# The recurrence inputs of a decoder step, made a second time by shifted columns of the stationary operand

## The chip, the cores and the metric

The kernel runs on one core of a Trainium2 chip. The metric is the device time of one execution in microseconds; the number given for a kernel is the median of its runs. All times below are microseconds (us) unless they are marked ns.

## What is computed

One layer of a hybrid decoder trunk, for a prompt of 1024 tokens and a decode batch of 8 sequences with 8 tokens each. A combined input projection feeds a dilated sliding-window attention and an S5 state-space group; their outputs are normalised, joined, projected, and a SwiGLU feed-forward part follows. The change is in the state-space part, which has 32 groups of 64 complex states and 16 channels each:

```python
def _cmul_combine(e1, e2):
    a1r, a1i, b1r, b1i = e1
    a2r, a2i, b2r, b2i = e2
    ...
    br = a2r * b1r - a2i * b1i + b2r
    bi = a2r * b1i + a2i * b1r + b2i
    return ar, ai, br, bi

def _s5(u, h0_re, h0_im, ...):
    ...
    bu_re = jnp.einsum('btgc,gnc->btgn', uf, bb_re)
    bu_im = jnp.einsum('btgc,gnc->btgn', uf, bb_im)
    ...
    _, _, h_re, h_im = lax.associative_scan(_cmul_combine, (a_r, a_i, bu_re, bu_im), axis=1)
    y = (jnp.einsum('btgn,gcn->btgc', h_re, c_re) - jnp.einsum('btgn,gcn->btgc', h_im, c_im) + d_skip * uf)
```

## The kernel before

The program has three phases. Phase A normalises the tokens, makes the input projection, and builds the tables of the state-space part. Phase B runs the prompt attention (`prompt_attn`) beside the recurrence (`ssm_main`), and after it the gate of the state-space output (`ssm_gate`) and the decode attention's values (`sample_values`). Phase E is the output projection and the feed-forward part, and takes more than half of the span.

Generators yield after each small step, and `merge` interleaves them by weights. That gives every instruction a priority; a scheduler then puts the instructions of each engine into a fixed order, engine by engine, with semaphores between engines. Every engine runs its own instructions in that order, and the DMA issues all stand in one queue, that of SyncE.

The recurrence runs over chunks of 8 tokens, 128 chunks of the prompt and 8 of the decode batch, so that an input tile U has 8 + 128 = 136 columns per group. Its 32 groups are 8 units u of 4 groups (one set of loads WI, WO, T, CS each), and each unit has two pairs m of 2 groups: 16 pairs. In SBUF and PSUM the 128 partitions hold the real rows (0 to 63) and the imaginary rows (64 to 127) of the states. A pair goes through five stages, one step apart, in `ssm_main`:

- `s0`: matmuls of the stationary WI (128 columns per group) with U give the chunk inputs in one PSUM bank px (tag `sd`, three banks for all users). The first pair of a unit also prepares HS on GpSimd.
- `s1`: ScalarE copies the 8 decode columns to xs (L928). VectorE multiplies the 128 prompt columns by a cosine table (L929, all 128 partitions), and by a sine table with real and imaginary rows exchanged, in two instructions on 64 partitions each (L930, L931). GpSimd subtracts (L932).
- `s2`: VectorE scans along the chunks (L940); GpSimd rotates back (L941 to L944).
- `s3`: the sum goes to HS (L948), on GpSimd or VectorE.
- `s4`: matmuls with T and WO give the outputs; ScalarE copies them to Y (L963).

All these matmuls have f32 operands, and each is recorded as two rows of weight load and two of matmul. `loads(u)` fetches the tables of a unit; WI has two buffers, so that the load of unit u waits for the last read of unit u - 2. Before the first load, the decode state is loaded in two halves through one buffer `hb`, transposed on PE and kept as h0. The line of every matmul is L75 (`mm1`), that of every transpose L79 (`tr`), of a load L82 and of a split L64 and L65, since helpers issue them.

The functions that the change touches, as the profile numbers their lines:

Of the kernel before, what the change touches and what calls it, by code (L numbers as in the profile page):

```python
# [10 lines left out]
F32 = mybir.dt.float32  # L11
F32R = mybir.dt.float32r
I32 = mybir.dt.int32
AF = mybir.ActivationFunctionType
OP = mybir.AluOpType
# [19 lines left out]
PB, VB, VSB, KKB, PTB, TAB, TCB, HSB, UB, CSB, WSB, HB = 10, 6, 4, 2, 2, 3, 2, 3, 2, 3, 5, 5  # L35
# [11 lines left out]
class K:  # L47
# [837 lines left out]
    def ssm_main(self, sp):  # L885
        nc, I, O = self.nc, self.I, self.O
        V, G = nc.vector, nc.gpsimd
        P8 = self.P8
        xs = sp.tile([128, 8, 32], F32, name="xs")
        hf = sp.tile([128, 32], F32, name="hf")  # L890
        WI, WO, T, CS, U, HS, Y, px, ta, tb, tcc = ({} for _ in range(11))

        def loads(u):
            if u >= 8:
                return
            q = u // 2
            if u % 2 == 0:
                U[q] = sp.tile([128, 8, 136], F32, tag="U", name="U", bufs=UB)
                self.load(U[q], self.dU[128 * q:128 * q + 128].rearrange("(g c) s t -> (c s) g t", c=16))
            WI[u] = sp.tile([128, 4, 128], F32, tag="WI", name="WI", bufs=2)  # L900
            WO[u] = sp.tile([128, 4, 128], F32, tag="WO", name="WO", bufs=3)
            T[u] = sp.tile([128, 4, 128], F32, tag="T", name="T", bufs=3)
            c = CS[u] = sp.tile([128, 2, 4, 128], F32, tag="CS", name="CS", bufs=CSB)
            self.load(WI[u], self.dWI[u])
            for h in range(2):
                self.load(c[64 * h:64 * h + 64].rearrange("p a g t -> p (a g t)"), self.dCS[q][64 * (u % 2):64 * (u % 2) + 64, h])
            self.load(T[u], self.dT[q][:, 4 * (u % 2):4 * (u % 2) + 4])
            self.first = self.load(WO[u], self.dWO[u])

        def s0(m):  # L910
            u, pr = divmod(m, 2)
            if pr == 0:
                HS[u] = sp.tile([128, 4, 138], F32, tag="HS", name="HS", bufs=HSB)
                G.memset(HS[u][:, :, 8:9], 0.0)
                G.tensor_scalar(HS[u][:, :, 0:8], h0[:, 0, :, 4 * u:4 * u + 4].rearrange("p b g -> p g b"), 1.0, 0.0, op0=OP.mult, op1=OP.add)
            px[m] = self.bank("sd")
            for j in range(2):
                g = 2 * pr + j
                self.mm1(px[m][:, 136 * j:136 * j + 136], WI[u][:, g], U[u // 2][:, 4 * (u % 2) + g])

        def s1(m):
            u, pr = divmod(m, 2)
            pxv = px[m][:, 0:272].rearrange("p (g c) -> p g c", g=2)
            co, si = CS[u][:, 0, 2 * pr:2 * pr + 2], CS[u][:, 1, 2 * pr:2 * pr + 2]
            a = ta[m] = sp.tile([128, 2, 128], F32, tag="ta", name="ta", bufs=TAB)
            b = tb[m] = sp.tile([128, 2, 128], F32, tag="tb", name="tb", bufs=TAB)
            g0 = 4 * u + 2 * pr
            nc.scalar.activation(xs[:, :, g0:g0 + 2].rearrange("p b g -> p g b"), pxv[:, :, 0:8], AF.Copy)  # L928
            V.tensor_tensor(a, pxv[:, :, 8:136], co, op=OP.mult)  # L929
            V.tensor_tensor(b[0:64], pxv[64:128, :, 8:136], si[64:128], op=OP.mult)  # L930
            V.tensor_tensor(b[64:128], pxv[0:64, :, 8:136], si[0:64], op=OP.mult)  # L931
            G.tensor_tensor(out=a, in0=a, in1=b, op=OP.subtract)  # L932

        def s2(m):
            u, pr = divmod(m, 2)
# [31 lines left out]

        h0 = sp.tile([128, 2, 8, 32], F32, name="h0")
        for half in range(2):
            hb = sp.tile([128, 3, 64], F32, tag="hb", name="hb", bufs=1)  # L970
            self.load(hb[:, 1], I["state_ssm_re"][0].rearrange("b g n -> (b g) n")[128 * half:128 * half + 128])
            self.load(hb[:, 2], I["state_ssm_im"][0].rearrange("b g n -> (b g) n")[128 * half:128 * half + 128])
            V.tensor_scalar(hb[:, 0], hb[:, 2], -1.0, None, op0=OP.mult)
            pt = self.bank("sd")
            self.tr(pt[:, 0:128], hb[:, 1:3].rearrange("p a n -> p (a n)"))
            self.tr(pt[:, 128:256], hb[:, 0:2].rearrange("p a n -> p (a n)"))
            nc.scalar.activation(h0[:, :, 4 * half:4 * half + 4].rearrange("p a b g -> p a (b g)"), pt[:, 0:256].rearrange("p (a c) -> p a c", a=2), AF.Copy)
        loads(0)
        yield 0
        for m in range(20):  # L980
            for k, f in enumerate((s0, s1, s2, s3, s4)):
                if 0 <= m - k < 16:
                    f(m - k)
            if m % 2 == 1:
                loads(m // 2 + 1)
            yield 3.0
# [1060 lines left out]
```

## Time and profile before

| | |
|---|---|
| median of three runs | 1548.5 us (1545.07 to 1552.62) |
| the profiled execution | 1555.69 us, of which the span is 1553.6 |
| granted TensorE clock, mean of the span | 0.939 of full speed |
| PE busy | 1439.5 us (93%) |
| PE weight loads busy | 1344.9 us (87%) |
| VectorE busy | 1090.4 us (70%) |
| ScalarE, GpSimd busy | 716.1 and 729.1 us (46%, 47%) |

PE is TensorE's matmul side and PEld its weight loads, DVE is VectorE, ACT ScalarE, POOL GpSimd, SP SyncE. A busy share is the time covered by recorded instructions. Matmuls are pipelined, so that a busy PE is not a PE at its peak; the distance between the starts of successive rows tells more. The granted clock is given as a share of 2.4 GHz; 0.50 is the lower level of 1.2 GHz. The recurrence stage discussed here lies between 316 and 446 us of the span.

### The profile page before, as it was taken

The page shows a single profiled execution, that of the slowest core. Times are in us where ns is not written, and L with a number is a line of the kernel's source. Part 1 is how long each engine was busy: PE and PEld are TensorE (multiplying, and loading weights), DVE is VectorE, ACT ScalarE, POOL GpSimd, SP SyncE. Part 2 cuts the span into 40 slices and gives each one's busy share as a digit, 9 for nine tenths or more (in the row PEclk, how much of TensorE's full clock was granted, in tenths as well). Part 3 has the DMA queues.
Part 4 walks back from the last instruction along what each step waited for, and adds up shares of the span by engine and source line. Part 5 has one row for each costly group of instructions (what it writes and reads, how often), then busy time and mean ns, then how long its engine had stood idle before and what let it go on. Part 6 is the DMA issues. An engine that isn't in the chain of part 4 may idle for free.

```text
span 1553.6 us, 28199 instructions
## 1 busy us (share of the span) xinstructions
PE 1439.5 (93%) x10005; PEld 1344.9 (87%) x10005; DVE 1090.4 (70%) x2226; ACT 716.1 (46%) x1815; POOL 729.1 (47%) x719
## 2 busy tenths in 40 slices
PE   5988987978889999999997999999999989999996
PEld 5987977966777677789987999999999989999996
DVE  6896399958867787787989555555555577579564
ACT  6233343435467667575444333333232365466443
POOL 3058445417735454410147678788774421113331
PEclk9998988968789999889998999999999999999998
DMA  8438887799676873444342276566564368689874
GB/s 215 160 120 279 242 241 220 209 214 224 179 189 180 206 182 89 127 146 128 108 131 80 84 214 212 175 205 196 184 197 141 108 248 294 195 297 324 238 234 126
DMA packets 244187, 292.90 MB, mean 189 GB/s; under 512 B 29870, under 2 KB 185358, under 8 KB 244046
## 3 DMA queue, kind: packets, MB, share of 16 engines
q1 hardware_dynamic: 244046, 291.10, 62.7%
q8 instruction: 79, 1.29, 0.4%
q14 instruction: 62, 0.51, 0.1%
HBM read 211.69 MB, written 79.35 MB: 187 GB/s over the span
## 4 chain that ended last, share of the span: by engine, by line
PE 60%; DVE 11%; DMA 7%; issue 4%; ACT 2%; POOL 1%; SPq 1%; POOLq 0%; DVEq 0%; ACTq 0%
PE pmm L72 15%; PE pmm L70 15%; PE pmm L71 15%; PE psd L75 5%; PE pmm L75 3%; PE ptr L79 2%; PE ppo L75 2%; DVE kk L682 1%; SPq L82 1%; DMA kk<-in_cache_attn_k_dram 1%; DVE ws L65 1%; PE ptr L75 1%; DMA hs<-dH 1%; DMA kf<-in_cache_attn_k_dram 1%; DVE hn L65 1%
## 5 line engine op out<-in xcount | busy, mean ns | idle before, releaser
L70 PE MATMUL pmm<-hn,ws 128*128 128x272 f32 x1232 | 359.1, 292 | 9.1 <-DVE u L1775 4.6
L72 PE MATMUL pmm<-hn,ws 128*128 128x272 f32 x1232 | 358.2, 291 | 2.1 <-DVE ws L65 2.1
L71 PE MATMUL pmm<-hn,ws 128*128 128x272 f32 x1232 | 356.9, 290 | 0.8 <-DVE hn L65 0.8
L64 ACT ACTIVATE ws<-wr 128x512 fp32r<-128x512 f32 (+2 forms) x238 | 151.8, 645 | 207.4 <-PE pmm L72 191.0
L70 PEld LDWEIGHTS pmm<-hn,ws 128*128 128x128 f32 x1232 | 234.1, 190 | 10.5 <-DVE u L1775 4.8
L65 DVE TENSOR_TENSOR ws<-wr,ws 128x512 fp32r<-128x512 f32 (+2 forms) x238 | 202.4, 857 | 52.7 <-ACT ws L64 51.3
L72 PEld LDWEIGHTS pmm<-hn,ws 128*128 128x128 f32 x1232 | 233.6, 190 | 2.9 <-DVE ws L65 2.7
L71 PEld LDWEIGHTS pmm<-hn,ws 128*128 128x128 f32 x1232 | 234.1, 190 | 1.3 <-DVE hn L65 1.2
L70 PE MATMUL pmm<-hs,ws 128*128 128x272 f32 x448 | 131.5, 294 | 5.1 <-DVE hid L1772 5.1
L72 PE MATMUL pmm<-hs,ws 128*128 128x272 f32 x448 | 131.2, 295 | 0.5 <-DVE ws L65 0.5
L71 PE MATMUL pmm<-hs,ws 128*128 128x272 f32 x448 | 131.3, 294 | 0.0
L1779 POOL TENSOR_TENSOR hid<-hid,s 128x272 f32<-128x272 f32 x88 | 82.2, 941 | 55.9 <-DVE hid L1772 52.0
L65 DVE TENSOR_TENSOR ws<-st,ws 128x512 fp32r<-128x512 f32 x72 | 60.6, 842 | 59.0 <-ACT ws L64 58.8
L828 POOL TENSOR_TENSOR vs<-vr,vs 128x512 fp32r<-128x512 f32 x40 | 56.0, 1406 | 85.3 <-ACT vs L826 75.1
L681 POOL TENSOR_TENSOR kf<-kf,qb 128x1024 f32<-128x1024 f32 x24 | 59.1, 2471 | 73.0 <-DMA kf<-in_cache_attn_k_dram 37.3
L70 PEld LDWEIGHTS pmm<-hs,ws 128*128 128x128 f32 x448 | 86.1, 192 | 5.3 <-ACT hs L64 5.3
L72 PEld LDWEIGHTS pmm<-hs,ws 128*128 128x128 f32 x448 | 85.5, 192 | 0.9 <-DVE ws L65 0.8
L71 PEld LDWEIGHTS pmm<-hs,ws 128*128 128x128 f32 x448 | 86.0, 192 | 0.0
L64 ACT ACTIVATE ws<-st 128x512 fp32r<-128x512 f32 x72 | 45.3, 629 | 81.0 <-PE pmm L72 69.9
L1125 DVE CUSTOM_DVE_ANT_0 P<-pmm,lnc 128x256 f32<-128x256 f32 (+1 forms) x128 | 47.4, 376 | 41.9 <-PE pmm L75 33.6
L70 PE MATMUL pmm<-mT,ws 128*128 128x272 f32 x256 | 74.5, 298 | 1.4 <-ACT ws L64 1.4
L71 PE MATMUL pmm<-mT,ws 128*128 128x272 f32 x256 | 74.9, 295 | 0.0
(441 smaller groups left out, 4088.3 us busy)
## 6 DMA issues: line engine op xcount, KB each, us to landing
vr<-in_cache_attn_v_dram SPq DMA_DIRECT2D x80, 256.0 KB
wr<-dS SPq DMA_DIRECT2D x32, 512.0 KB
hs<-dH SPq DMA_DIRECT2D x28, 544.0 KB
kf<-in_cache_attn_k_dram SPq DMA_DIRECT2D x48, 256.0 KB
wr<-in_ffn_w_gate_dram SPq DMA_DIRECT2D x24, 512.0 KB
wr<-in_ffn_w_up_dram SPq DMA_DIRECT2D x24, 512.0 KB
wx<-dS SPq DMA_DIRECT2D x24, 512.0 KB
dH<-hid SPq DMA_DIRECT2D x22, 544.0 KB
```

The costliest lines, as they stand in the source:

```text
L64: self.nc.scalar.activation(hi, src, AF.Copy)
L65: (eng or self.nc.vector).tensor_tensor(out=lo, in0=src, in1=raw(hi), op=OP.subtract)
L70: nc.tensor.matmul(out, lhsT=wh, rhs=xh, start=start, stop=False)
L71: nc.tensor.matmul(out, lhsT=wh, rhs=xl, start=False, stop=False)
L72: nc.tensor.matmul(out, lhsT=wl, rhs=xh, start=False, stop=stop)
L75: self.nc.tensor.matmul(out, lhsT=w, rhs=x, start=start, stop=stop)
L79: self.nc.tensor.transpose(out, in_, self.ident[:n, :n])
L82: return self.nc.sync.dma_start(out=out, in_=in_).ins
L681: nc.gpsimd.tensor_tensor(out=kf[i], in0=kf[i], in1=qb[b][:, 0:1].to_broadcast((128, 2, 512)), op=OP.mult)
L828: eng.tensor_tensor(out=s[:, 1], in0=vr[i], in1=raw(s[:, 0]), op=OP.subtract)
L1125: V.tensor_tensor_reduce(out=P[h, g].rearrange("p b k -> p (b k)")[:, o:o + n], in0=s[:, o:o + n], in1=lnc[:, part, 256 - n:256], scale=-1 ...
L1779: self.mark = G.tensor_tensor(out=o, in0=o, in1=sb, op=OP.mult).ins
```

## The change

The input matmuls of a pair are made twice. WI gets 64 more columns per group, a copy of its first 64, made by ScalarE in SBUF once per unit. Columns 0 to 127 are the stationary operand of the first product, as before; columns 64 to 191 are that of the second, whose output has real and imaginary rows exchanged. Both products cover the 128 prompt columns alone and lie side by side in one PSUM bank of 512 columns. VectorE then multiplies each by its table on all 128 partitions, and GpSimd adds where it subtracted. The 8 decode columns get matmuls of their own, four per unit, in a bank of their own, with one ScalarE copy per unit instead of one per pair. The tile `hb` moves into the slots of the tag `ta`, of which there are three, so that the two halves have a slot each.

```diff
-            WI[u] = sp.tile([128, 4, 128], F32, tag="WI", name="WI", bufs=2)
+            WI[u] = sp.tile([128, 4, 192], F32, tag="WI", name="WI", bufs=2)
...
-            self.load(WI[u], self.dWI[u])
+            self.load(WI[u][:, :, 0:128], self.dWI[u])
...
                 G.tensor_scalar(HS[u][:, :, 0:8], h0[:, 0, :, 4 * u:4 * u + 4].rearrange("p b g -> p g b"), 1.0, 0.0, op0=OP.mult, op1=OP.add)
+                nc.scalar.activation(WI[u][:, :, 128:192], WI[u][:, :, 0:64], AF.Copy)
+                p = self.bank("sd")
+                for g in range(4):
+                    self.mm1(p[:, 8 * g:8 * g + 8], WI[u][:, g, 0:128], U[u // 2][:, 4 * (u % 2) + g, 0:8])
+                nc.scalar.activation(xs[:, :, 4 * u:4 * u + 4].rearrange("p b g -> p g b"), p[:, 0:32].rearrange("p (g b) -> p g b", g=4), AF.Copy)
+
             px[m] = self.bank("sd")
-            for j in range(2):
-                g = 2 * pr + j
-                self.mm1(px[m][:, 136 * j:136 * j + 136], WI[u][:, g], U[u // 2][:, 4 * (u % 2) + g])
+            for k in range(2):
+                for j in range(2):
+                    g = 2 * pr + j
+                    self.mm1(px[m][:, 256 * k + 128 * j:256 * k + 128 * j + 128], WI[u][:, g, 64 * k:64 * k + 128], U[u // 2][:, 4 * (u % 2) + g, 8:136])
...
-            pxv = px[m][:, 0:272].rearrange("p (g c) -> p g c", g=2)
+            pxv = px[m].rearrange("p (k g c) -> p k g c", k=2, g=2)
...
-            g0 = 4 * u + 2 * pr
-            nc.scalar.activation(xs[:, :, g0:g0 + 2].rearrange("p b g -> p g b"), pxv[:, :, 0:8], AF.Copy)
-            V.tensor_tensor(a, pxv[:, :, 8:136], co, op=OP.mult)
-            V.tensor_tensor(b[0:64], pxv[64:128, :, 8:136], si[64:128], op=OP.mult)
-            V.tensor_tensor(b[64:128], pxv[0:64, :, 8:136], si[0:64], op=OP.mult)
-            G.tensor_tensor(out=a, in0=a, in1=b, op=OP.subtract)
+            V.tensor_tensor(a, pxv[:, 0], co, op=OP.mult)
+            V.tensor_tensor(b, pxv[:, 1], si, op=OP.mult)
+            G.tensor_tensor(out=a, in0=a, in1=b, op=OP.add)
...
-            hb = sp.tile([128, 3, 64], F32, tag="hb", name="hb", bufs=1)
+            hb = sp.tile([128, 2, 128], F32, tag="ta", name="hb", bufs=TAB).rearrange("p a (b n) -> p (a b) n", n=64)
```

## Rows read from the trace of the kernel before

**Rows 1.** The page: the chain that ended last, share of the span by engine.
```profile
PE 60%; DVE 11%; DMA 7%; issue 4%; ACT 2%; POOL 1%; SPq 1%; POOLq 0%; DVEq 0%; ACTq 0%
```
**Rows 2.** Windows: length; PE, PEld, DVE, ACT, POOL busy (instructions); clock, DMA share, GB/s.
```profile
335.00:355.00 20.00, 15.58 (x66) 12.79 (x65) 13.38 (x35) 6.68 (x23) 8.56 (x14) 0.59 1.07 232
355.00:375.00 20.00, 17.57 (x93) 14.34 (x93) 19.51 (x62) 9.32 (x35) 16.61 (x26) 0.86 0.84 200
375.00:395.00 20.00, 20.00 (x117) 16.64 (x114) 16.01 (x55) 12.26 (x42) 12.22 (x24) 0.91 0.80 221
395.00:415.00 20.00, 16.14 (x84) 13.69 (x84) 18.16 (x52) 6.62 (x24) 16.21 (x27) 0.83 0.87 221
415.00:432.00 17.00, 16.79 (x60) 13.00 (x60) 11.66 (x32) 9.29 (x26) 10.94 (x19) 0.50 0.60 147
```
**Rows 3.** Waits, 335 to 440 us: us in total, times, longest.
```profile
PE psd L75 <- DMA WI<-dWI: 6.1, 1, 6.1
PE psd L75 <- DVE tb L940: 3.3, 1, 3.3
PE pmm L75 <- DVE ST L1125: 0.6, 2, 0.4
```
**Rows 4.** Groups by line, 335 to 432 us: busy, mean ns, idle before and releaser.
```profile
L931 DVE TENSOR_TENSOR tb<-psd,CS 64x256 f32<-64x256 f32 x16 | 6.7, 417 | 0.2
L929 DVE TENSOR_TENSOR ta<-psd,CS 128x256 f32<-128x256 f32 x16 | 6.6, 411 | 1.4 <-ACT xs L928 1.1
L928 ACT ACTIVATE xs<-psd 128x16 f32<-128x16 f32 x16 | 3.1, 193 | 10.3 <-PE psd L75 10.3
```
**Rows 5.** Timeline of VectorE: start, us, instruction.
```profile
347.90 0.42 DVE L1125 CUSTOM_DVE_ANT_0 P<-pmm,lnc 128x256 f32<-128x256 f32 x1
...
348.25 0.42 DVE L1125 CUSTOM_DVE_ANT_0 P<-pmm,lnc 128x256 f32<-128x256 f32 x1
...
389.25 0.42 DVE L930 TENSOR_TENSOR tb<-psd,CS 64x256 f32<-64x256 f32 x1
389.69 0.42 DVE L931 TENSOR_TENSOR tb<-psd,CS 64x256 f32<-64x256 f32 x1
```
**Rows 6.** Timeline of PE's matmuls, with the idle time before in brackets.
```profile
356.68 1.25 PE L75 MATMUL psd<-U,WI 128*128 128x136 f32 x4 [6.10 <-DMA WI<-dWI]
357.72 0.66 PE L75 MATMUL psd<-U,T 128*128 128x136 f32 x2
...
396.31 0.68 PE L75 MATMUL psd<-U,WI 128*128 128x136 f32 x4
396.75 0.98 PE L75 MATMUL ppo<-PT,VS 128*128 128x128 f32 x7
```
**Rows 7.** The tile WI: count, ns minimum/median/maximum, first and last start.
```profile
L75 PE MATMUL psd<-U,WI x64: 277/407/594, 334.1 to 411.5; 128*128 128x136 f32 x64
```
**Rows 8.** Timeline of PE's weight loads for selection matmuls of 16 columns.
```profile
311.11 1.42 PEld L75 LDWEIGHTS psd<-sel,Z 128*128 128x128 f32 x12
...
339.07 1.82 PEld L75 LDWEIGHTS psd<-sel,Z 128*128 128x128 f32 x12
```
**Rows 9.** Timeline of ScalarE.
```profile
329.53 0.50 ACT L1135 ACTIVATE P<-P,ST 128x256 f32<-128x256 f32 x1
```
**Rows 10.** Timeline of SyncE's queue around the loads of hb.
```profile
322.12 1.82 SPq L82 DMA_DIRECT2D CS<-dCS  x2
328.65 0.34 SPq L82 DMA_DIRECT2D hb<-in_state_ssm_re_dram  x1
```
**Rows 11.** Windows of 2 us, with the columns of the second group.
```profile
326.00:328.00 2.00, 2.00 (x5) 1.25 (x5) 1.52 (x6) 1.97 (x3) 0.00 (x0) 0.50 1.11 291
328.00:330.00 2.00, 2.00 (x6) 1.27 (x5) 0.73 (x4) 2.00 (x9) 0.00 (x0) 0.50 0.46 111
...
338.00:340.00 2.00, 2.00 (x13) 1.60 (x12) 1.12 (x6) 0.98 (x5) 1.92 (x5) 1.00 1.06 141
340.00:342.00 2.00, 2.00 (x12) 2.00 (x11) 0.29 (x1) 0.25 (x2) 0.84 (x2) 0.50 1.07 221
```

## The prediction

> **What bounds the kernel now.** I read the chain of work that ended last first. Over the whole span TensorE (PE) carries 60% of it and VectorE (DVE) 11% [rows 1]. The change touches one stage, the recurrence (`ssm_main`) running beside the prompt attention from about 334 to 446 us, so I read the busy times by 20 us next [rows 2]. From 355 on PE is busy 17.6, 20.0, 16.1 and 16.8 us of 20, 20, 20 and 17. VectorE is nearly as full in two of the four (19.5 and 18.2). Both are candidates, and what decides is who waits. The waits of the stage [rows 3] show PE losing 6.1 us once to a load of WI and 3.3 us once to VectorE, and 0.6 us to score statistics. Apart from those two gaps its starts follow one another. So PE sets the pace here, VectorE is a close second, and after 446 us PE goes on as the carrier of phase B: what delays the last matmul of the recurrence delays the end. The granted clock matters too: PE ran at 0.59, 0.86, 0.91, 0.83 and 0.50 of full speed in the five stretches [rows 2], that is partly at 1.2 and partly at 2.4 GHz.
>
> **VectorE, removed.** Per pair of groups (16 pairs m) three products of 0.41 to 0.43 us [rows 4] (L930 is as L931) become two on all 128 partitions: a half product on 64 partitions costs as much as a whole one, so one of three goes. By duration that is 16 x 0.42 = 6.7 us. Starts tell more: L930 to L931 is 0.44, while an operation on all partitions followed by another such one is 0.35 apart (347.90 to 348.25) [rows 5]. Three at 0.44 against two at 0.35 is 0.62 a pair, 9.9 us in all. I take 9 us of VectorE time, between 6.7 and 9.9.
>
> The Trainium skill, "VectorE: DVE Perf Modes", section "Two Vector instructions with no wait between them", says that an instruction which starts on another partition quadrant than the one before is held until all earlier ones have finished. The starts in [rows 5] agree with it; by durations alone the saving would be 6.7 us, by this rule 9.9.
>
> What of it reaches the end? Only what PE waits for VectorE: 3.3 us at 399.9, and about 1 us in pieces [rows 3]. The 3.3 us stand right behind the load of U for the last units, so they may be a transfer in truth. I credit 2.5 us, between 0 and 4.5.
>
> **TensorE, added.** Each pair has two matmuls of 136 columns now, recorded as four rows, two for each f32 matmul. It will have four of 128 columns, eight rows. From the first row of such a group to the next group is 0.44 us at full clock (396.31 to 396.75), thus 0.11 a row, and 1.04 at half clock (356.68 to 357.72), thus 0.26 [rows 6]. Four rows more, with the old four 6% narrower, cost 0.43 at full and 0.9 at half clock.
>
> Once per unit (8 units of two pairs) come four matmuls of 8 columns, eight rows, for the decode tokens. Nearest are the selection matmuls of 16 columns with the same 128-column stationary operand: twelve weight loads, which follow one another without a break, take 1.42 us at full clock (at 311.11), 0.12 a row, and 1.82 (at 339.07), 0.15 a row, in a stretch whose clock falls to half [rows 8]. Eight cost 0.95 or 1.2.
>
> Where do they fall? Sixteen groups of input matmuls run from 334.1 to 411.5 [rows 7].
> - Pairs 0 to 3, units 0 and 1, lie ahead of the 6.1 us gap, at half clock: 4 x 0.9 + 2 x 1.2 = 6.0 us. PE then reaches the gap 6.0 us later and stands 0.1 us in it: free, if the load that ends it stays where it is. If that cover were gone, 6.0 us.
> - Pairs 4 to 15, units 2 to 7, lie behind it. Measured by the same spacing, 8 pairs and 4 units stand at full clock, 4 pairs and 2 units at half: 8 x 0.43 + 4 x 0.9 + 4 x 0.95 + 2 x 1.2 = 13.2 us, with PE back to back around them. All on the path.
>
> Bounds: 10.9 us if everything ran at full clock (12 x 0.43 + 6 x 0.95), 18.0 if all at half (12 x 0.9 + 6 x 1.2).
>
> **ScalarE.** Sixteen copies of 0.19 us [rows 4] become eight; eight copies of 128x256 from SBUF come, each near the 0.50 of the exponential of that shape, which reads and writes SBUF [rows 9]. Net 8 x (0.50 + 0.20) - 16 x 0.19 = +2.5 us on an engine that is busy at most 12.3 of 20 us in any of these stretches [rows 2]: nothing on the path, hidden behind PE. The copy of WI adds a wait: ScalarE must wait for that load, and the exponentials behind it in its queue wait with it, then PE's second half of the products. Where WI lands late (before 356.68) PE waits for the same load anyway. VectorE no longer waits for the small copy out of the same bank (1.1 us in all) [rows 4]. I set these against each other: 0, between -1 and +2.
>
> **PSUM banks.** The three `sd` banks rotate; each unit takes one more, freed by a ScalarE copy. VectorE holds a bank until its products are done, so PE can meet an occupied bank sooner: +1 us, between 0 and 4 (half a microsecond a unit).
>
> **Loads.** The second load of `hb` no longer reuses one slot. The queue of SyncE stood after its CS loads (323.94) until 328.65 for it [rows 10]; T, WO, WI, CS and the values behind it may start up to 4.7 us sooner. But the transfers were busy 1.11 of their share just before and 0.46 after [rows 11], so only the hole can be filled: 2 us sooner for the loads that follow, and the WI load that ends the 6.1 us gap is one of them. Against it, WI now lands in rows of 512 B with gaps in place of 2 KB; nothing in the trace prices that alone. At the 200 to 232 GB/s of the stretch [rows 2] 256 KB take 1.2 us; between nothing and twice that, so up to 1.2 us a load. I take 1 us sooner in sum; since the 6.0 us of PE work ahead of the gap leave 0.1 us of it, almost all of this gain shows only as loads that wait less, and at most 2 us could come off. `hb` itself in slots of `ta`, and `add` for `subtract` on GpSimd, cost nothing: same shapes, and the slots are idle then.
>
> **Sum.** +13.2 (PE) - 2.5 (VectorE relief) + 1 (bank) + 0 (ScalarE) - 1 (loads, and the attention's values in them) = +10.7 us, 0.7%. The profiled execution took 1555.7 us with a span of 1553.6, 0.5% above the median of 1548.5; with the sum it would be 1566.4, and the median 1559.2. I predict 1559.
>
> **Rivals.**
> 1. **PE has room.** In the same stretches weight loads fill only 12.8 to 16.6 of 20 us [rows 2], so the added rows might slip into slots that the recorded matmul time hides, or the clock might stay up in 415 to 432, where 17 us ran at half. Against it: starts are evenly spaced at 0.11 a row with nothing between. If so, the 13.2 us shrink to about 3 and the median is 1548.5 + 3 - 2.5 = 1549. Chance 0.24. The Trainium skill, page "Trainium Kernel Development and Optimization", section "Performance Expectations", says that matmul busy time is a bad metric because matmuls are pipelined, and that the busy share of weight loads is a good one. By that rule this rival would be the forecast.
> 2. **VectorE is the bound.** VectorE is busy 19.5 and 18.2 of 20 us in two stretches [rows 2], and the one 3.3 us wait names it [rows 3]. If it decides, 9 us come off and PE's work hides in its waits (6.1 + 3.3): 1548.5 - 9 = 1539.5. Against it: PE waits for it so little. Chance 0.10.
> 3. **The clock falls.** The matmuls of 8 columns are thin. In the stage before, the one stretch of thin matmuls (from 339.07) [rows 8] was followed by a granted clock that went from 1.00 to 0.50 within 2 us, with PE recorded busy throughout [rows 11]. If each thin group took PE down, the full-clock stretches of the stage, some 30 us, would pay up to half again: +15 on top, 1574. It decides once two or more such stretches turn. Chance 0.13. It ends on the slow side, as the forecast.
> 4. **It does not free VectorE**, because the full product from the second half of a bank is slower than 0.35. Then the relief is lost and the median is 1561; counted within the forecast.
>
> **How the numbers follow.** Forecast (1553 to 1566) 0.53, rival 1 0.24, rival 2 0.10, rival 3 0.13. A measurement here tells about 0.5% from no change, so same is 1540.8 to 1556.2. Slower: most of the forecast (0.45) and rival 3 (0.13), 0.58. Same: the rest of the forecast (0.08) and rival 1, 0.32. Faster: rival 2, 0.10. The range runs from 1546, the low side of rival 1, to 1575, which takes in rival 3's centre; it leaves out rival 2 and the tails, under 2 in 10.
>
> **What would show it.** Right: VectorE has 32 product rows of 128x256 in place of 48 and some 9 us less; PE has 128 rows of input matmuls and 64 thin ones; the last input matmul lies 10 us or so later with the gap before 356 nearly closed; everything behind shifts by as much. Wrong: the PE rows of the stage closer than 0.11 apart, a granted clock that differs over long stretches of it, or a reordering of the attention's work elsewhere that moves more than the stage itself.

## The result and the profile after

The changed kernel takes 1568.8 us (median of four runs, 1561.15 to 1571.51) beside 1550.2 of the kernel before. The ratio is put at 1.0094 with a 95% interval of 1.0066 to 1.0122, that is 14.6 us slower (10 to 19); the medians of these few runs lie further apart, 18.6 us. Seven more runs, beside 30 of the kernel before, gave 1563.85 against 1552.75, ratio 1.0082 (1.0047 to 1.0118). The prediction was 1559 in a range of 1546 to 1575, 10.7 us over the median of before, with slower as the likeliest sign. Sign and size came about as forecast: 10.7 lies inside 10 to 19. Below, some terms of the sum turn out to be of other sizes, and they do not simply add.

The profiled execution took 1567.98 us, its span 1566.2, mean granted clock 0.934. Of its page, the busy time of each engine (answers the table of before) and the shares of the chain that ended last [rows 1]:

```profile
PE 1464.7 (94%) x10133; PEld 1367.7 (87%) x10133; DVE 1084.1 (69%) x2210; ACT 720.2 (46%) x1815; POOL 732.7 (47%) x719
...
PE 69%; DVE 12%; DMA 8%; issue 4%; ACT 2%; POOL 2%; SPq 1%; POOLq 0%; DVEq 0%; ACTq 0%
```

PE has 128 matmul rows more than the 10005 of before and is busy 25 us longer; VectorE has 16 instructions fewer and is busy 6.3 us less. The windows of the stage, with the columns of [rows 2]:

```profile
335.00:355.00 20.00, 15.46 (x64) 13.57 (x64) 12.54 (x32) 6.16 (x18) 9.29 (x12) 0.51 1.01 213
355.00:375.00 20.00, 20.00 (x79) 17.02 (x79) 9.63 (x37) 6.07 (x21) 11.34 (x17) 0.55 0.52 133
375.00:395.00 20.00, 18.18 (x99) 15.62 (x97) 14.30 (x48) 10.08 (x36) 13.80 (x27) 0.83 0.63 161
395.00:415.00 20.00, 19.59 (x123) 16.32 (x121) 16.75 (x57) 10.94 (x34) 12.93 (x21) 0.97 0.50 145
415.00:435.00 20.00, 20.00 (x110) 18.11 (x110) 13.34 (x34) 9.35 (x30) 15.03 (x27) 0.77 0.81 214
```

VectorE is no longer nearly full anywhere: in the second window it went from 19.5 to 9.6 us of 20. (The windows are the same stretches of time, not the same work, since the stage has moved.) PE is busy 18.2 to 20.0 of 20 us in each window from 355 on. What waits for what, from the waits of PE between 316 and 475 us (as [rows 3]) and the groups by line of the same stretch (as [rows 4]: count, busy time, mean ns, then the idle time before and who ended it):

```profile
PE pmm L75 <- DMA KH<-dK: 5.4, 1, 5.4
PE psd L75 <- issue: 3.4, 1, 3.4
PE psd L75 <- DMA U<-dU: 1.4, 1, 1.4
PE psd L75 <- DVE tb L936: 1.2, 1, 1.2
PE pmm L75 <- DVE ST L1130: 1.0, 3, 0.4
```
```profile
L75 PE MATMUL psd<-U,WI 128*128 128x128 f32 x128 | 27.5, 370 | 1.2 <-DVE tb L936 1.2
...
L75 PE MATMUL psd<-U,WI 128*128 128x8 f32 x64 | 13.1, 330 | 4.8 <-issue 3.4 <-DMA U<-dU 1.4
L935 DVE TENSOR_TENSOR ta<-psd,CS 128x256 f32<-128x256 f32 x16 | 6.6, 414 | 12.4 <-PE psd L75 12.2
L936 DVE TENSOR_TENSOR tb<-psd,CS 128x256 f32<-128x256 f32 x16 | 6.6, 413 | 0.0
L917 ACT ACTIVATE WI<-WI 128x256 f32<-128x256 f32 x8 | 3.3, 412 | 10.0 <-DMA WI<-dWI 10.0
L921 ACT ACTIVATE xs<-psd 128x32 f32<-128x32 f32 x8 | 1.8, 221 | 5.1 <-PE psd L75 5.1
```

The wait for KH opens the stage and stood there before too (6.4 us). Of the waits behind it, the 6.1 us for WI and the 3.3 us for VectorE no longer stand under these names; the other four lines come to 7.0 us, 4.8 of them ahead of thin matmuls. The 3.4 us that end on "issue" are in all likelihood still the wait for WI: ScalarE's copy of that WI, which had waited for the load, begins in the same moment. From the timelines of PE and of ScalarE (the sixteen rows are eight of 8 columns and eight of 128):

```profile
352.22 3.76 PE L75 MATMUL psd<-U,WI 128*128 128x8 f32 x16 [3.38 <-issue]
```
```profile
352.21 0.42 ACT L917 ACTIVATE WI<-WI 128x256 f32<-128x256 f32 x1 [4.85 <-DMA WI<-dWI]
```

And the direction has turned: VectorE's first product (L935) now waits 12.2 us in all for the product that PE makes. In [rows 4] the product on all partitions had 1.4 us of idle time before it, none of it put down to PE. Of the tile `psd` (ns minimum/median/maximum, first and last start, as [rows 7]), the input products and the last products of the recurrence:

```profile
L75 PE MATMUL psd<-U,WI x192: 172/361/581, 327.4 to 438.1; 128*128 128x128 f32 x128, 128*128 128x8 f32 x64
...
L75 PE MATMUL psd<-HS,WO x64: 278/281/594, 357.3 to 459.9; 128*128 128x136 f32 x64
```

Before, the input products ran from 334.1 to 411.5 [rows 7]. The last products of the recurrence before, and the first score product of the stage, before and then after:

```profile
L75 PE MATMUL psd<-HS,WO x64: 278/279/541, 358.5 to 446.6; 128*128 128x136 f32 x64
```
```profile
323.61 0.76 PE L75 MATMUL pmm<-KH,QS 128*128 128x128 f32 x2 [6.38 <-DMA KH<-dK]
```
```profile
318.28 0.76 PE L75 MATMUL pmm<-KH,QS 128*128 128x128 f32 x2 [5.38 <-DMA KH<-dK]
```

So in these two profiles the stage starts 5 us earlier and ends 13 us later, as much as the whole span grew (12.6 us): the loss is made between these two places, and passes on to the end unchanged (1107.0 us behind the last product before, 1106.3 after). The order of the instructions within the stage is also another one: the kernel's scheduler reorders when work is added, and the loads have changed places too. That is a confounder for every run below.

### The profile page after: what moved, and what is told of

It reads as the page before. It is cut to its first block, busy times and chain, and to the rows that moved or that the text cites. A ratio compares the mean times of both kernels' runs of the same rounds, so it can differ in the third digit from the quotient of the medians.

```text
span 1566.2 us, 28451 instructions
## 1 busy us (share of the span) xinstructions
PE 1464.7 (94%) x10133; PEld 1367.7 (87%) x10133; DVE 1084.1 (69%) x2210; ACT 720.2 (46%) x1815; POOL 732.7 (47%) x719
## 4 chain that ended last, share of the span: by engine, by line
PE 69%; DVE 12%; DMA 8%; issue 4%; ACT 2%; POOL 2%; SPq 1%; POOLq 0%; DVEq 0%; ACTq 0%
PE pmm L70 16%; PE pmm L72 16%; PE pmm L71 16%; PE psd L75 9%; PE pmm L75 4%; PE ppo L75 3%; PE ptr L79 3%; DMA kk<-in_cache_attn_k_dram 2%; DVE ws L65 2%; DVE kk L682 1%; PE ptr L75 1%; SPq L82 1%; DMA wr<-in_w_in_dram 1%; DVE Sm L689 1%; DVE hn L65 1%
## 5 line engine op out<-in xcount | busy, mean ns | idle before, releaser
L681 POOL TENSOR_TENSOR kf<-kf,qb 128x1024 f32<-128x1024 f32 x24 | 63.1, 2641 | 67.1 <-DMA kf<-in_cache_attn_k_dram 27.8
```

The source lines that it names most:

```text
L681: nc.gpsimd.tensor_tensor(out=kf[i], in0=kf[i], in1=qb[b][:, 0:1].to_broadcast((128, 2, 512)), op=OP.mult)
```

## Experiments

Each variant is compared with the kernel before. The table gives what was measured, and every ± in this document is a 95% interval; "equal clock" is worked out below it.

| run | rows added to PE | median, us | ratio to before (95%) | mean clock | at equal clock, us |
|---|---|---|---|---|---|
| change, 4 and 7 runs | 64 + 64 thin | 1568.8, 1563.9 | 1.0094, 1.0082 | 0.9353 | +12.9 ± 2.0 |
| e1_thin | 64 thin | 1555.0 | 1.0031 (1.0002 to 1.0061) | 0.9359 | +4.1 ± 1.9 |
| e2_double | 64 | 1552.3 | 1.0005 (0.9978 to 1.0032) | 0.9381 | +2.3 ± 2.0 |
| e3_hb | 0 | 1553.4 | 1.0009 (0.9977 to 1.0041) | 0.9348 | -1.0 ± 2.0 |
| e4_oldvec | 64 + 64 thin | 1569.8 | 1.0112 (1.0069 to 1.0154) | 0.9335 | +13.3 ± 2.7 |
| e5_vec | 0 | 1551.8 | 0.9997 (0.9972 to 1.0022) | 0.9343 | -1.3 ± 2.0 |
| e8_double_oldvec | 64 | 1556.6 | 1.0030 (1.0011 to 1.0049) | 0.9342 | +3.3 ± 2.0 |
| e9_two_banks | 64 | 1551.4 | 0.9998 (0.9972 to 1.0024) | 0.9377 | +1.9 ± 2.0 |
| e10_wide | 64 + 64 widened | 1557.3 | 1.0043 (1.0017 to 1.0070) | 0.9418 | +12.0 ± 2.1 |
| e11_thin_wide | 64 widened | 1561.7 | 1.0064 (1.0039 to 1.0089) | 0.9334 | +6.8 ± 2.5 |
| e12_wide_attn | 0 | 1555.6 | 1.0024 (1.0000 to 1.0048) | 0.9397 | +7.4 ± 2.0 |
| e13_late | 64 + 64 thin | 1564.2 | 1.0092 (1.0063 to 1.0121) | 0.9312 | +10.0 ± 2.7 |

**Equal clock.** The runs of one kernel scatter by 4 to 5 us, and every run records its mean granted clock. One straight line through the runs of the table, with a level of its own for each kernel and 92 runs of the kernel before (mean clock 0.9361), has a slope of 0.96 ± 0.13 us for each 0.001 of mean clock; around it the runs scatter by 3.2 us. The last column is the distance of a kernel's level from that of before on this line. It takes out what a run won or lost by its clock; it does not say why the clock was what it was. The ± covers the scatter of the runs, not what another order of the same work would change.

### The parts one at a time: e1_thin and e2_double

e1: the kernel before with the decode columns in thin matmuls of their own.

```
+                p = self.bank("sd")
+                for g in range(4):
+                    self.mm1(p[:, 8*g:8*g+8], WI[u][:, g], U[u//2][:, 4*(u%2)+g, 0:8])
+                nc.scalar.activation(xs[...4 groups...], p[:, 0:32], AF.Copy)
...
-                self.mm1(px[m][:, 136*j:136*j+136], WI[u][:, g], U[...])
+                self.mm1(px[m][:, 128*j:128*j+128], WI[u][:, g], U[..., 8:136])
...
```

> The kernel before, with one part of the change alone: the 8 decode columns of each unit go through four matmuls of their own in a bank of their own and one ScalarE copy a unit; the product of 128 columns is made once, and VectorE's three products and everything else stay as before. Theory A (the loss is TensorE's added rows, each kind of them at its own price): the change's trace shows a four-row group of 8 columns at 0.4 us at the full clock and at 0.8 at half, the 136 columns become 128, which gives back 0.02 us a row, and the first two units lie in the gap ahead of WI(2): six units times 0.4 to 0.9, so 2 to 6 us slower than before. Rival B (the clock falls because of thin matmuls): over 8 us slower than before, and the granted clock of the stretch from 340 to 375 falls as in the change (0.55 where before showed more). Rival C (the scheduler's other order of the whole stage makes the loss, not these instructions): the time is not tied to the rows added, so anything from no difference to the change's +18.

e2: the changed kernel without them; it leaves out the decode columns, whose place is filled from the initial states.

```
-                (bank, four thin matmuls, copy)
+                nc.scalar.activation(xs[...4 groups...], HS[u][:, :, 0:8], AF.Copy)
```

> The changed kernel without the thin matmuls: the decode columns are not made (their place is filled by a ScalarE copy of the same size from the initial states, so the decode states are not the reference's); the doubled product, the 192-column operand and VectorE's two products stay. Theory A: the change's loss less that of the thin groups: 64 rows of 128 columns instead of none, 48 of them past the gap, at 0.11 to 0.23 us, 5.3 to 11 us, less VectorE's relief of 0 to 4.5: 4 to 11 us slower than before, and 4 to 9 us faster than the changed kernel. Rival B: within 4 us of the time before, since nothing is thin. Rival C: not tied to the rows.

Measured: e1 1.0031, 4.8 us slower; e2 1.0005, 0.8 us. For e1 theory A's 2 to 6 held, rival B's "over 8" did not, and the mean clock was that of the kernel before. For e2, A's 4 to 11 was too much, and B's "within 4 us" held, though any account in which this part is cheap would have given that. The surprise is the sum: 4.8 + 0.8 is less than half of the change's 13 to 15. So what has to be explained is why two additions that are cheap alone are dear together.

### The staging tile alone: e3_hb

```
-            hb = sp.tile([128, 3, 64], F32, tag="hb", bufs=1)
+            hb = sp.tile([128, 2, 128], F32, tag="ta", bufs=TAB).rearrange(...)
```

> The kernel before with only the initial states' staging tile moved into the slots of the first products, so that SyncE no longer holds the loads behind it. Theory A: the loads of the second unit come earlier, and TensorE's 6.1 us wait for WI at the start of the recurrence stays, for it is WI of the third unit (two buffers): 0 to 2 us faster than before. Rival C: any difference over 4 us, either sign, shows that an edit that adds no work reorders the stage and moves the time by itself.

1.0009, no difference that can be told: neither a gain of the earlier loads nor a loss by reordering alone.

### Does VectorE's relief pay? e4_oldvec, e5_vec, e8_double_oldvec

e4: all of the change's PE work, and VectorE's three old products.

```
-            V.tensor_tensor(b, pxv[:, 1], si, op=OP.mult)
-            G.tensor_tensor(out=a, in0=a, in1=b, op=OP.add)
+            V.tensor_tensor(b[0:64], pxv[64:128, 0], si[64:128], op=OP.mult)
+            V.tensor_tensor(b[64:128], pxv[0:64, 0], si[0:64], op=OP.mult)
+            G.tensor_tensor(out=a, in0=a, in1=b, op=OP.subtract)
```

> The changed kernel with VectorE's three products and GpSimd's subtraction of the kernel before, read from the first product of each bank (the second is made and not read): all of TensorE's added work, none of VectorE's relief. Theory A (TensorE is what ends the stage, VectorE waits for it): 0 to 3 us slower than the changed kernel, 18 to 22 slower than before. Rival D (VectorE ends the stage, and the relief is worth its 6.7 us): 6 to 9 us slower than the changed kernel. Rival C: not tied.

e5: the kernel before with two products instead of three, from the one product of PE. It leaves out the exchange of real and imaginary rows.

```
-            V.tensor_tensor(b[0:64], pxv[64:128, :, 8:136], si[64:128], op=OP.mult)
-            V.tensor_tensor(b[64:128], pxv[0:64, :, 8:136], si[0:64], op=OP.mult)
+            V.tensor_tensor(b, pxv[:, :, 8:136], si, op=OP.mult)
```

> The kernel before with VectorE's work of the change and none of TensorE's: b is one product of 128x256 straight from the bank, without the exchange of the halves (the recurrence's inputs are wrong by that). 16 VectorE instructions and some 6.7 us of engine time go. Theory A (VectorE's part is worth 0 to 4.5 us here): 0 to 4.5 faster than the kernel before. Rival D (VectorE ends the stage): 6 to 9 faster. If it is within 1 us of the kernel before, no version that only frees VectorE here can gain.

e8: e2 with the three old products (the edit of e4).

> The doubled product alone, without thin matmuls (decode columns filled by a ScalarE copy from the initial states, so the decode states are not the reference's) and with VectorE's three products of the kernel before, which read the first product only. It stands to the doubled run as the run with the old products stands to the changed kernel. If TensorE's idle time takes up the doubled product: 0 to 5 us slower than the kernel before, within 3 of the doubled run. If it is VectorE's relief that pays for the doubled product: 6 to 9 us slower than the kernel before.

Giving VectorE its old work back costs 1.0112 against 1.0094 or 1.0082 (e4), 1.0030 against 1.0005 (e8); taking it away from the kernel before brings nothing (e5, 0.9997). At equal clock the three differences are 0.4, 1.0 and 1.3 us, each ± 2 to 3. The relief is there on VectorE, the groups by line of e4 show what was given back, 6.8 + 6.7 + 6.7 us instead of 6.6 + 6.6:

```profile
L936 DVE TENSOR_TENSOR tb<-psd,CS 64x256 f32<-64x256 f32 x16 | 6.8, 426 | 0.2
L935 DVE TENSOR_TENSOR ta<-psd,CS 128x256 f32<-128x256 f32 x16 | 6.7, 418 | 13.6 <-PE psd L75 13.6
L937 DVE TENSOR_TENSOR tb<-psd,CS 64x256 f32<-64x256 f32 x16 | 6.7, 418 | 0.2
```

but with all three VectorE still waits for PE, 13.6 us in all: it is not the engine that is late. Rival D falls: 6 to 9 us were expected in all three, and at equal clock none is near it, though the plain ratios of e8 (1.0030 against 1.0005, 4 us) leave room for some part.

### The change without thin matmuls, nothing left out: e9_two_banks

```
+            px[m] = [self.bank("sd"), self.bank("sd")]
+            (first product: 136 columns into bank 0; second: 128 columns into bank 1)
+            nc.scalar.activation(xs[...2 groups...], pxv[:, :, 0:8], AF.Copy)
```

> The changed kernel with the thin matmuls gone and nothing left out: the first product keeps its 136 columns (decode columns included, copied out a pair at a time as before) in one bank, the second of 128 columns goes to a bank of its own. Against the changed kernel it has 64 TensorE rows fewer and 8 columns more in 64, and takes one PSUM bank more per pair. Theory A' (TensorE's idle time of some 13 us takes up the first such addition and not the second): within 5 us of the kernel before, as the run without thin matmuls was, 9 to 16 faster than the changed kernel. A theory in which banks matter: the second bank a pair makes products wait, and it is 5 or more slower than the kernel before.

0.9998: as fast as the kernel before, and by the ratios 0.8% or some 13 us faster than the change (11.0 ± 2.7 at equal clock), in line with e2. That a bank more per pair costs anything is not seen. PE's waits between 320 and 470 us and its busy time:

```profile
PE pmm L75 <- DVE ST L1131: 2.9, 5, 1.3
PE ptr L79 <- ACT P L1182: 2.9, 1, 2.9
PE psd L75 <- DMA U<-dU: 0.7, 1, 0.7
```
```profile
PE 1459.4 (94%) x10069; PEld 1363.0 (88%) x10069; DVE 1084.0 (70%) x2210; ACT 721.8 (47%) x1823; POOL 734.6 (47%) x719
```
```profile
L75 PE MATMUL psd<-U,WI x128: 272/421/594, 326.9 to 425.4; 128*128 128x136 f32 x64, 128*128 128x128 f32 x64
...
L75 PE MATMUL psd<-HS,WO x64: 279/279/434, 353.7 to 446.4; 128*128 128x136 f32 x64
```

PE is busy 20 us longer than in the kernel before (part of it at a lower clock, 0.932 in this profile), but the 6.1 and 3.3 us gaps of [rows 3] are not there, and the recurrence ends at 446.4, where it ended before. It is the fastest complete version with the change's idea in it, and no better than the kernel before.

### Is it the clock? e10_wide, e11_thin_wide, e12_wide_attn

e10 and e11 make the thin matmuls of the change and of e1 128 columns wide:

```
-                    self.mm1(p[:, 8*g:8*g+8], WI[u][:, g, 0:128], U[..., 0:8])
+                    self.mm1(p[:, 128*g:128*g+128], WI[u][:, g, 0:128], U[..., 0:128])
...
```

> The changed kernel with the 64 thin matmuls made 128 columns wide (the same rows and weight loads; 120 of the 128 columns are not read). Theory A (a row costs its weight load, 0.10 to 0.12 us at the full clock and twice that at half, whatever its columns): 0 to 2 us slower than the changed kernel and the mean clock the same. Rival B (the clock is lower for the thin columns): the mean clock rises by 0.002 or more towards that of the kernel before, and the time is 2 to 5 us faster than the changed kernel, although TensorE does more.

> The run with the thin matmuls alone on the kernel before, with these 64 matmuls made 128 columns wide (120 of them not read): the same pair as the changed kernel and its wide form, one step away. Rival B' (wide rows hold the clock up, here as there): mean clock 0.939 to 0.942 against 0.936 of the thin run, and 3 to 7 us faster than that, so 3 us faster to 1 slower than the kernel before. If the wide form of the changed kernel had its clock by chance of the order of work: clock 0.934 to 0.937 and 0 to 3 us slower than the thin run.

e12 widens the thin matmuls of the attention phase of the kernel before (with one ScalarE copy more per two samples):

```
-                self.mm1(p[:64, 128:136], QB[...], self.KN[:, f, 8*b:8*b+8], ...)
+                self.mm1(p[:64, 128:192], QB[...], self.KN[:, f, 0:64], ...)
-                self.mm1(p[:, 16*j:16*j+16], Z[:, j], asel)      (and bsel, 32 columns)
+                self.mm1(p[:, 48*j:48*j+48], Z[:, j], sel[:, 12:60])
...
```

> The kernel before, in which the thin matmuls of the attention phase (8, 16 and 32 columns) are made 64 and 48 columns wide, with the columns that are needed copied out (the same rows, one ScalarE copy more per two samples). If wide columns hold the clock up wherever they stand: the half-clock stretch from 323 to 360 is shorter, mean clock 0.939 or more, 2 to 6 us faster than the kernel before. If it is the stage's idle time and not its thin rows that brings the clock down: no change within 2 us.

e10 did what rival B foretold: more columns, clock 0.9418, 6 us faster than the change (1557.3 against 1563.9). e11, the same edit on e1, did the contrary: clock 0.9334, 1.0064 against 1.0031, more than either account had given it. So the width of these matmuls does not set the clock in general. At equal clock e10 stands at +12.0, beside the change's +12.9: its gain is a gain of clock, and whether that came from the columns or from the other order of work is not settled. e12 raised the clock a little, to 0.9397, as foretold if wide columns hold it up, but the 2 to 6 us of gain did not come: it is 1.0024, 4 us slower. Its profiled execution, the slowest of its twelve, shows longer waits; of PE's waits between 320 and 470 us:

```profile
PE pmm L75 <- DVE ST L1126: 8.8, 7, 2.9
PE psd L79 <- DMA hb<-in_state_ssm_im_dram: 5.3, 1, 5.3
PE psd L75 <- ACT P L1136: 3.5, 1, 3.5
```

The first was 1.4 us in the kernel before over the same stretch. An edit in one phase went with other waits in the next: +7.4 us at equal clock with no row added. That the waits are the whole of it is not shown.

### Does the place matter? e13_late

```
 def s0(m):  -  (bank, four thin matmuls, copy)
 def s1(m):  +  if pr == 1: (the same, behind VectorE's products)
```

> The changed kernel with each unit's thin matmuls and their copy made one step later, behind the second pair's products instead of ahead of the first pair's. Theory A (TensorE is what ends the stage, so its rows cost the same wherever they stand): within 3 us of the changed kernel. Rival E (the thin group's price on top of the doubled product, about 13 us, is that it stands between the weights' landing and the products for which VectorE waits): 5 to 10 us faster than the changed kernel.

1.0092, as the change itself (at equal clock 10.0 beside 12.9, within the uncertainty). The thin group is not dear because it stands ahead of the first product; rival E's 5 to 10 us are not there.

### The change again: after_again

> The changed kernel once more, in more runs, beside the others on one chip: 1567 to 1569 and a mean clock of 0.932 to 0.934, where the kernel before has 0.936. If more runs bring its clock to 0.936 and its time below 1564, the part of the loss put down to the clock was chance.

1563.85, and a mean clock of 0.9369 in these seven runs: both better than foretold, so that the low clock of the first four (0.9325, worth some 3.5 us) was chance. The mean clock of all eleven runs of the change is 0.9353 ± 0.0019, that of the kernel before 0.9361 ± 0.0008. At 0.96 us per 0.001 the difference is 0.8 us of 13.7 (mean of eleven runs against 92). The change's loss is not a loss of clock. The second profile, 1560.7 us of span, ends the recurrence 7 us after that of before, and is itself 7 us longer; it has the same rows with less of the half clock:

```profile
L75 PE MATMUL psd<-U,WI x192: 172/361/582, 326.6 to 432.0; 128*128 128x128 f32 x128, 128*128 128x8 f32 x64
...
L75 PE MATMUL psd<-HS,WO x64: 278/279/535, 355.9 to 453.7; 128*128 128x136 f32 x64
```

### What the runs say together

Take the levels at equal clock. None of the change's rows: -1.0 and -1.3 (e3, e5). One set of 64 rows: 1.9, 2.3, 3.3, 4.1, 6.8 (e9, e2, e8, e1, e11), mean 3.7. Both sets: 10.0, 12.0, 12.9, 13.3 (e13, e10, change, e4), mean 12.1. On this scale the groups do not overlap (the nearest, 6.8 and 10.0, lie within each other's uncertainty), whatever VectorE does, however wide the rows are and wherever they stand; by the plain ratios e11 (1.0064) lies above e10 (1.0043). That PE's added rows make the loss is shown to this extent: taking away either set takes away most of it, in variants whose orders of work differ. One run stands outside the groups: e12 has none of these rows and +7.4 ± 2.0, so another order of work can by itself move a kernel by as much as a set of rows.

How the loss divides is less sure. By the means the second 64 rows cost 8.4 us, more than twice the first. e1 and e2 add up to 6.4, and the change lies 6.5 ± 3.3 above that. With the wide rows, e11 and e2 add up to 9.1 beside 12.0 of e10, and that difference (3.0 ± 3.7) is not told from nothing.

PE's own work is a second measure. Summing busy time times granted clock over windows of 2 us (PE's work in us of full clock) gives 1370.4 for the profile of before, 1381.7 and 1381.6 for the two of the change, +11.2 for 128 rows or 0.09 a row. One set adds 3.0 to 6.0 (e8, e9, e1, e2, e11), mean 4.3, beside 3.7 us of time; both sets add 8.8 to 14.5 (e13, e4, the change twice, e10), mean 11.0, beside 12.1. The sum is uncertain by some 4 us: e5 and e12, with as many rows as before, give 3.8 less. By this measure the time follows PE's work, and the first set is not clearly cheaper than the second.

PE's idle time (span less busy time) falls from 114.1 to 101.5 and 100.5 us with both sets; with one set it is 91.4 (e9), 99.0 (e1), 100.2 (e2) and 103.5 (e8), already as low. That is what one would see if one set of rows lies in PE's waits and a second finds them taken. It is a reading, not a proof: e5, with no row added, also has only 103.9.

## Why the prediction was right, point by point

- **PE sets the pace, VectorE is a close second.** Right. VectorE now waits 12.2 us for PE (L935), and e4, e5 and e8 moved the time by 0.4 to 1.3 us at equal clock.
- **VectorE's relief: 9 us of engine time, 2.5 on the path.** The engine time is 6.9 by durations (6.6 + 6.8 + 6.7 in the stretch of the profile of before, 6.6 + 6.6 after), and the starts agree with the larger figure: two products on all partitions start 0.35 and 0.33 us apart, and 0.33 ahead of an instruction that is ready, against 0.44 [rows 5]. Only the value of it was high: 0.4 to 1.3 measured, not told from nothing, and inside the 0 to 4.5 given.

  In VectorE's timeline of after, two pairs of products:

```profile
388.64 0.42 DVE L935 TENSOR_TENSOR ta<-psd,CS 128x256 f32<-128x256 f32 x1 [1.90 <-PE psd L75]
388.99 0.41 DVE L936 TENSOR_TENSOR tb<-psd,CS 128x256 f32<-128x256 f32 x1
...
394.19 0.42 DVE L935 TENSOR_TENSOR ta<-psd,CS 128x256 f32<-128x256 f32 x1
394.52 0.41 DVE L936 TENSOR_TENSOR tb<-psd,CS 128x256 f32<-128x256 f32 x1
394.85 0.55 DVE L794 TENSOR_TENSOR Z<-S,sel 128x384 f32<-128x384 f32 x1
```

  The spacing is what the Trainium skill, "VectorE: DVE Perf Modes", section "Two Vector instructions with no wait between them", would have it (an instruction that begins on another partition quadrant is held); the trace agrees, with 0.35 against 0.44. It is worth little here, since PE and not VectorE is late.
- **The price of a row.** Right for the products, mis-sized for the thin ones. PE's timeline of after; the price is the distance from a group to the next one:

```profile
365.47 1.71 PE L75 MATMUL psd<-U,WI 128*128 128x8 f32 x8
367.04 0.56 PE L75 MATMUL pmm<-KH,QS 128*128 128x256 f32 x1
...
369.06 2.08 PE L75 MATMUL psd<-U,WI 128*128 128x128 f32 x8
370.93 0.43 PE L75 MATMUL psd<-U,T 128*128 128x136 f32 x1
...
374.24 1.16 PE L75 MATMUL psd<-U,WI 128*128 128x128 f32 x8
375.23 0.40 PE L75 MATMUL psd<-U,T 128*128 128x136 f32 x2
...
424.94 0.51 PE L75 MATMUL psd<-U,WI 128*128 128x8 f32 x4
425.30 0.36 PE L75 MATMUL ppo<-PT,VS 128*128 128x256 f32 x1
```

  Eight products of 128 columns: 1.87 us at half clock and 0.99 at full, 0.23 and 0.12 a row, near the 0.26 and 0.11 of [rows 6]. A pair's four rows more thus cost 0.83 at half clock and 0.55 at full, where 0.9 and 0.43 were forecast (by its own 0.11 a row and the narrower columns the second should have been 0.39). Eight thin rows: 1.57 at half, 0.20 a row, and 0.09 at full. They had been priced at 1.2 for eight at half (0.15 a row, from a stretch whose clock changed in its middle, so too low) and 0.95 at full (0.12 a row, too high). A row of 8 columns thus costs about three quarters of one of 128 at full clock, and five sixths at half.
- **Units 0 and 1 are free, 13.2 us on the path.** Half right, and the total owes something to luck. Counted from the first score product of the stage, PE reached the gap after 27.0 us before (323.61 to 350.58) and after 30.6 us in the profile after (318.28 to 348.84): 3.6 us later and not 6.0, because three of the sixteen pairs of score products that stood ahead of the gap now stand behind it. WI came 0.9 us later by the same count, and 3.4 us of the gap remain (at 352.22) where 0.1 had been foretold. So part of the gap was filled, and part of what the first two units added was only moved on. Behind the gap, it was thought that all would be paid. The single parts came out below their sums: the doubled product with no relief 3.3 ± 2.0 (e8) against 7.0; with relief 2.3 ± 2.0 (e2) against 4.5; the thin groups 4.1 ± 1.9 (e1) against 6.2. The two together came out at 12.9 ± 2.0 against 10.7. The sum fits the change as a whole; as a sum of parts it does not hold, and why it does not stays open.
- **ScalarE 0, bank +1, loads -1.** None shows in a time by itself: e3 (the staging tile alone) gave 1.0009, and e9, with a bank more for every pair, 0.9998. PE's wait of 1.2 us for VectorE's second product (L936) fits the bank term of 1; it is argued, not tested. ScalarE's copy of WI waits 10.0 us in all for its load (L917); in one place PE waits out the same load (352.21 and 352.22 above), and no wait of PE names the copy itself.
- **Rival 1, PE has room.** It fits the doubled product alone (e2 1.0005, e9 0.9998), the thin groups alone less (e1 1.0031), and it is wrong for both together. The Trainium skill, "Trainium Kernel Development and Optimization", "Performance Expectations", would judge by the busy share of weight loads: 12.8 to 16.6 of 20 us before [rows 2], 13.6 to 18.1 after. By that rule there was room. One set of 64 rows did cost little (3.7 us on the mean); the second cost 8.4 although the weight loads never filled a window.
- **Rival 2, VectorE is the bound.** Wrong: 1539.5 was named, and e5 (VectorE relieved and nothing added) gave 0.9997.
- **Rival 3, the clock falls.** Wrong for the loss as a whole: 0.8 of 13.7 us. Two relatives with the same thin rows did have a lower clock, 0.9335 (e4) and 0.9312 (e13), worth 2.5 and 4.7 us on the line. The stage held some 44 us of full clock (from 0.86, 0.91 and 0.83 of 20 us each [rows 2]) and not 30, so the rival's +15 was a low figure. In the one profile after, the half clock did last longer in one place (0.55 from 355 to 375, where before had 0.86 [rows 2]), and was given back in others (0.97 from 395 to 415 against 0.83). A single profile would have misled here: only the many runs show that the means are alike.
- **The signs to look for.** 32 product rows on VectorE and 128 + 64 rows on PE came; the last input matmul stands at 438.1 in place of 411.5, 27 us later and not 10, since the scheduler moved attention work ahead of it (from the start of the stage, 48 pairs of score products stand ahead of it instead of 41, and 64 products of P with V instead of 46); the recurrence's end (13 and 7 us later in the two profiles) was the better sign for the change. A reordering of the stage, named as a sign against, did occur.

## What to carry to other kernels

Cost an addition to the engine that sets the pace as a whole, not only part by part: here two parts that cost 0.3% and 0.05% alone cost 0.8 to 0.9% together. One possible reason, not proven, is that the first rows lie in that engine's waits and the next find them taken. Work taken from an engine that waits for another may be worth next to nothing until that other is relieved; here a VectorE saving of 7 us bought about 1, not told from 0. In this kernel a matmul of 8 columns cost three quarters to five sixths of one of 128 with the same stationary operand, so decode columns were best left as extra columns of a product that is made anyway, even at the price of a PSUM bank (e9 against the change).

## What the runs showed of the hardware

- The time of a run goes with its granted clock: 0.96 ± 0.13 us for each 0.001 of the mean, which leaves 3.2 us of scatter where there were 4.4 (92 runs of the kernel before). If all the time were PE's, 0.001 would cost 1.66 us (an estimate: 1553.6 us times 0.001 over 0.936), so about 60% of that shows at the end. Where the rest goes is not shown.
- The same 64 rows made wider went with a clock 0.0065 higher in one kernel and 0.0025 lower in another (e10, e11). What decides this in a given order of work stays open.
- An edit that adds no row can go with 4 us by the times and 7 us at equal clock (e12). With a scheduler that reorders, one variant alone says little below some 5 us.
